# Second mixer of a two-layer decoder trunk: q and k stored in thirds of 32 dimensions, four heads' scores in four quadrants and four PSUM banks, and ScalarE's function tables requested at other places

## The chip, the cores and the metric

The kernel runs on one core of a Trainium2 chip. A core has five engines that run side by side: TensorE (PE: matmuls, and PEld: its weight loads), VectorE (DVE), ScalarE (ACT), GpSimd (POOL) and SyncE (SP), which issues most of the DMAs. Matmuls write to PSUM, which has eight banks of 512 fp32 values for each of 128 partitions. The metric is the device time of one execution in microseconds (us). The kernel before has a median of 994.5 us over 3 runs (994.04 to 995.5).

## The reference, cut to what matters

One sequence of 256 tokens with 1024 features goes through two layers. Each layer is a half-step SwiGLU FFN, a token mixer and another half-step FFN, all with RMSNorm and a shift, scale and gate computed from a condition vector. The first layer's mixer is a block-sparse attention with 16 heads of 64 dimensions and a table of position biases. The second layer's mixer, which the change is about, is a latent attention:

```python
def mla_attention(h, w_dq, q_a_norm_g, w_uq, q_g, w_o, k, v, positions):
    q = (rms_norm(h @ w_dq, q_a_norm_g) @ w_uq).reshape(B, S, MLA_HEADS, MLA_QK)   # 16 heads of 96
    q = rms_norm(q, q_g)
    q = jnp.concatenate([q[..., :MLA_NOPE], rope(q[..., MLA_NOPE:], positions)], axis=-1)   # 64 + 32
    o = causal_block_attention(q, k, v, MLA_QK ** -0.5)
    return o.reshape(B, S, MLA_HEADS * MLA_V) @ w_o
```

The k of a head is built in the same way: 64 dimensions from a latent, 32 position dimensions that all heads share, an RMSNorm over the 96 with gain k_g, and a rotation of the last 32. Scores are q·k over 96 dimensions with a causal mask, softmax runs in fp32, and the output is the weighted sum of v with 64 dimensions a head.

## The kernel before

All activations stay in on-chip memory; only weights are streamed, by SP's queue. Weights and activations are split into a high and a low part in a reduced fp32 format (`fp32r`), and each product is three matmuls: high by high, low by high, high by low (`mm3`, L774 to L776; in most of the FFN L974 and L982). `split` (L644 on ACT, L645 on DVE) makes the two parts of each weight tile. Attention's own matmuls (scores, weighted sum, transposes) are plain fp32, which the chip runs as two instructions for each matmul in the source; transposes are one.

The source text does not give the order of the instructions. Each engine's order comes from a planner in the kernel (`Order`, L250 to L535): it gives every instruction a cost (`duration`, L203), simulates the five engines, and fixes the sequence that each engine then runs strictly in order. So a change of one instruction's cost or buffer can move others.

The second mixer is `mla` (L1408). It works through the 16 heads in four groups of four (`GH` = 4, `NG` = 4), each over the two tiles of 128 query tokens (`t` = 0, 1):

- `proj` makes q for the group (L1483, 128x384), and k and v (L1496, 128x512), into tiles of the ring `mm` (4 banks). `head_rstd` (L1123: ACT L1126, DVE L1129 and L1130, POOL L1131) gives each head's inverse norm; DVE writes the normed heads to `qn` and `kn` (L1486, L1500, L1501), laid out as token x (head, 96), and `rope_apply` rotates the last 32 dimensions.
- `to_T` (L1461) transposes each head on PE (L1466: 128x96 to 96x128, 8 for q and 8 for k in a group) and ACT copies the result with the head gain as a scale for each partition to `qT` and `kT` (L1467).
- `attention` (L1011) is shared by both mixers; `bias is not None` (`halves`) marks the first. `scores` in the second mixer makes three banks of the ring `tr` (3 banks, `at_tile`): one with the four heads' 128x128 scores of tile 0, and two with two heads' 128x256 scores of tile 1. A score is one matmul with 96 rows (L1036); the causal mask is added as a bf16 matmul for each bank (L1037). DVE takes each bank's row maxima (L1050), ACT the exponentials with their sums (L1061), DVE normalises (L1066, L1067).
- `transposes` (L1076) turns the probabilities on PE and ACT copies them (L1078); `av` (L1096) is the weighted sum, two heads side by side in the array's columns, into another bank of `tr`; `split_evac` (L789, L790) writes it out as `oT`.
- `out_proj` (L1107) multiplies `oT` with the output weights.

In the first mixer, scores have 64 rows: the even heads lie on partitions 0 to 63 and the odd ones on 64 to 127, and two heads' matmuls go to different banks (L1041). The ring `ada` (1 bank, `ps_ada`) holds sums for the adaLN gates (L703, L704).

ACT needs a table of functions for Silu and another one for Exp. A load (`ACT_TABLE_LOAD`) stands in the program ahead of the first instruction that needs the other table: Exp's before the first exponential of each mixer (L1061) and Silu's before the first Silu of the FFN after each mixer (L939).

## Time and profile before

The profiled execution took 994.78 us; its span from the first to the last instruction is 993.0 us, and about 1.8 us lie around it.

| Part of the kernel | us from the span's start, about |
|---|---|
| first FFN, with the start and the bias tables | 0 to 213 |
| first mixer | 213 to 328 |
| second FFN | 328 to 514 |
| third FFN (second layer) | 514 to 700 |
| second mixer: latents | 700 to 727 |
| second mixer: four groups of heads | 727 to 790 |
| second mixer: rest of the output projection | 790 to 802 |
| last FFN | 802 to 993 |

The page of a profile lists busy time by engine, the chain of work that ended last (followed backwards from the last instruction), and groups of instructions. A timeline's rows are: start and duration in us, engine, line, operation, output and inputs, how many were merged into the row, and in brackets the idle time before it with what ended it. PE's matmuls overlap in their pipeline, so what one costs is read from start to start and not from its duration.

### The profile page before, as it was taken

What the parts mean: (1) busy time and instruction counts of PE and PEld (TensorE: products, weight loads), DVE (VectorE), ACT (ScalarE), POOL (GpSimd) and SP (SyncE); (2) the same over time, 40 slices, a digit from 0 to 9 for tenths busy, and PEclk for the clock granted to TensorE, in tenths of its full rate; (3) what the DMA queues carried; (4) which work ended last, traced back from release to release, by engine and by line L of the source; (5) the groups of instructions that cost most, each with busy time, mean ns of one, the idle gap of its engine ahead of it and who ended that gap; (6) DMA issues with size and microseconds to landing.
All of it is one profiled execution on the core that took longest, in us unless ns stands there. A gap on an engine that the chain in (4) does not pass through costs nothing.

```text
span 993.0 us, 15266 instructions
## 1 busy us (share of the span) xinstructions
PE 979.3 (99%) x5570; PEld 831.1 (84%) x5573; DVE 842.0 (85%) x1433; ACT 623.1 (63%) x1168; POOL 79.9 (8%) x120
## 2 busy tenths in 40 slices
PE   8999999999999999999999999999999999999998
PEld 7988888878887788888888888888878878888886
DVE  8999999799999999999799999744999789677542
ACT  5698564379665966555367665633879696657421
POOL 1012100012231100000010000000143010000000
PEclk9999999999999999999999999999999999999999
DMA  9978989798887789888989998452343467444630
GB/s 367 408 272 277 363 304 341 288 349 319 297 303 279 250 320 346 321 314 307 366 298 353 351 332 292 171 214 89 106 154 127 171 233 306 181 170 172 230 128 22
DMA packets 53275, 260.55 MB, mean 262 GB/s; under 512 B 6192, under 2 KB 6736, under 8 KB 35024
## 3 DMA queue, kind: packets, MB, share of 16 engines
q1 hardware_dynamic: 51696, 255.93, 70.4%
q0 software_dynamic: 1024, 3.17, 1.0%
q8 instruction: 44, 0.72, 0.3%
q10 hardware_dynamic: 480, 0.47, 0.2%
q14 instruction: 31, 0.25, 0.1%
HBM read 255.36 MB, written 4.19 MB: 261 GB/s over the span
## 4 chain that ended last, share of the span: by engine, by line
PE 84%; DVE 7%; ACT 3%; DMA 3%; issue 1%; POOL 1%; ACTq 0%; SPq 0%; DVEq 0%; POOLq 0%
PE mm L974 23%; PE mm L774 14%; PE mm L775 13%; PE mm L776 13%; PE mm L982 12%; DVE lo L645 3%; DMA raw<-in_first_dram 2%; PE at L1096 1%; PE at L1076 1%; PE at L1036 1%; DMA bias_d<-bt 1%; ACT hi L644 1%; PE at L1041 1%; PE tr L824 1%; PE mm L1623 1%
## 5 line engine op out<-in xcount | busy, mean ns | idle before, releaser
L645 DVE TENSOR_TENSOR lo<-raw,hi 128x1024 fp32r<-128x1024 f32 (+3 forms) x312 | 370.3, 1202 | 79.4 <-ACT hi L644 63.2
L644 ACT ACTIVATE hi<-raw 128x1024 fp32r<-128x1024 f32 (+3 forms) x312 | 318.0, 1038 | 146.9 <-PE mm L776 119.6
L974 PE MATMUL mm<-h,hi 128*128 128x512 f32 x1120 | 288.1, 393 | 0.0
L974 PEld LDWEIGHTS mm<-h,hi 128*128 128x128 f32 x1120 | 199.7, 189 | 34.6
L982 PEld LDWEIGHTS mm<-h,lo 128*128 128x128 f32 x1120 | 155.2, 190 | 12.7 <-DVE lo L645 0.8
L982 PE MATMUL mm<-h,lo 128*128 128x256 f32 x1120 | 162.3, 283 | 0.1
L655 DVE CUSTOM_DVE_ANT_0 adaw<-adaw,c_b,cols 128x1024 f32<-128x1024 f32 x112 | 141.8, 1280 | 3.3 <-DMA adaw<-in_ada_dram 2.3
L774 PE MATMUL mm<-hi,gh 128*128 128x512 f32 x352 | 137.3, 390 | 0.0
L775 PE MATMUL mm<-lo,gh 128*128 128x512 f32 x352 | 137.1, 389 | 0.0
L776 PE MATMUL mm<-hi,gl 128*128 128x512 f32 x352 | 137.1, 389 | 0.0
L774 PE MATMUL mm<-hi,h 128*128 128x512 f32 (+1 forms) x240 | 94.1, 399 | 0.8 <-ACT h L789 0.8
L775 PE MATMUL mm<-lo,h 128*128 128x512 f32 (+1 forms) x240 | 93.2, 393 | 0.0
L776 PE MATMUL mm<-hi,h 128*128 128x512 f32 (+1 forms) x240 | 92.9, 395 | 0.1
L776 PEld LDWEIGHTS mm<-hi,gl 128*128 128x128 f32 x352 | 66.1, 188 | 13.7
L774 PEld LDWEIGHTS mm<-hi,gh 128*128 128x128 f32 x352 | 66.1, 188 | 13.4
L775 PEld LDWEIGHTS mm<-lo,gh 128*128 128x128 f32 x352 | 66.1, 188 | 13.3
L693 DVE SCALAR_TENSOR_TENSOR acc<-adaw,cols,acc 128x1024 f32<-128x1024 f32 x48 | 61.5, 1281 | 0.1
L774 PEld LDWEIGHTS mm<-hi,h 128*128 128x128 f32 x240 | 45.0, 188 | 10.9 <-ACT h L789 1.9
L912 ACT ACTIVATE g<-mm 128x256 f32<-128x256 f32 x70 | 26.4, 377 | 43.7 <-PE mm L982 41.7
L776 PEld LDWEIGHTS mm<-hi,h 128*128 128x128 f32 x240 | 45.0, 188 | 9.5 <-DVE h L790 0.8
L775 PEld LDWEIGHTS mm<-lo,h 128*128 128x128 f32 x240 | 45.1, 188 | 7.7 <-issue 0.2
L912 ACT ACTIVATE u<-mm 128x256 f32<-128x256 f32 x70 | 26.4, 377 | 34.5 <-PE mm L982 34.3
(233 smaller groups left out, 1228.5 us busy)
## 6 DMA issues: line engine op xcount, KB each, us to landing
raw<-in_w_dram SPq DMA_DIRECT2D x142, 1024.0 KB, 5.4
adaw<-in_ada_dram SPq DMA_DIRECT2D x160, 512.0 KB, 5.5
raw<-in_w_dram SPq DMA_DIRECT2D x12, 512.0 KB, 3.6
raw<-in_first_dram SPq DMA_DIRECT2D x7, 512.0 KB, 9.0
raw<-in_w_dram SPq DMA_DIRECT2D x6, 576.0 KB, 3.7
bias_d<-bt SPq DMA_DIRECT2D x12, 256.0 KB, 4.9
bg<-bias_d POOLq DMA_DIRECT2D x4, 768.0 KB, 7.1
raw<-in_first_dram SPq DMA_DIRECT2D x10, 256.0 KB, 9.0
```

What stands on the lines that cost most here:

```text
L644: nc.scalar.activation(hi, src, AF.Copy)
L645: nc.vector.tensor_tensor(lo, src, hi.bitcast(F32), op=ALU.subtract)
L655: nc.vector.tensor_tensor_reduce(wt, wt, c_b, 1.0, cols[:, i, c:c + 1], op0=ALU.mult, op1=ALU.add, accum_out=m_cols[:, i, c:c + 1])
L693: nc.vector.scalar_tensor_tensor(acc, ada_tile(j, k), cact[:, k:k + 1], acc, op0=ALU.mult, op1=ALU.add)
L774: nc.tensor.matmul(ps, lh, rh, start=start, stop=False)
L775: nc.tensor.matmul(ps, lh, rl, start=False, stop=False)
L776: nc.tensor.matmul(ps, ll, rh, start=False, stop=stop)
L824: nc.tensor.transpose(kslice(pt, j), kslice(y, j), ident)
L912: nc.scalar.activation(x, ps[:, S:], AF.Copy)
L974: nc.tensor.matmul(ps[i], w[0], hs[2], start=k == 0, stop=False)
L982: nc.tensor.matmul(ps[i][:, S:], w, hk_, start=False, stop=k == KD - 1)
L1036: nc.tensor.matmul(ps3[:, i, :], qTs(e, t), kTs(e, nk), start=i == 0, stop=False)
```

## The change

- `qn` and `kn` are laid out as token x (third, head, 32) in place of token x (head, 96). A transpose then takes one third of all four heads at once (128x128): head e's 32 dimensions land on partitions 32e to 32e+31, its own quadrant. There are 6 transposes for q and 6 for k in a group, where there were 8 and 8.
- ACT's copies after the transposes: for q three of 128x256 (two with a scale for each partition, one with a constant), for k one of 128x512 and one of 128x256 without a gain. Both gains of the first 64 dimensions are multiplied into q's scale once, ahead of time, in one instruction.
- A score is now three matmuls with 32 rows each, one for each third, summed in PSUM: 24 matmuls in a group in place of 8. The four heads follow each other, each in its own quadrant and its own bank (three of the ring `tr`, the fourth from `mm`), with both query tiles side by side in a head's bank. The mask is added once for each bank, 128x256, four in a group in place of three.
- DVE takes the maxima of a bank by blocks of 128 keys (128x384, four in a group), and two small minima join the two blocks of tile 1 (the values are negated).
- `av` writes to the ring `ada` in place of `tr`, in both mixers.
- A new helper `table` runs one 128x1 activation with scale 0 for its table alone: Exp after the last units of the first FFN of each layer, Silu after the last `av` of each mixer.
- The planner's costs know fp32 matmuls with at most 32 rows (a quarter of the time), and it keeps consecutive ones in their order.

```diff
@@ duration
             c = 2 * max(112.0, cols / 1.2 + 2.5)
-            if DH in (aps[-1].ap[0][1], aps[0].ap[0][1]):
+            rows = aps[0].ap[0][1]
+            if rows <= 32:
+                c /= 4
+            elif DH in (aps[-1].ap[0][1], rows):
                 c /= 2
@@ Order.add
-            half = type(i).__name__ == "InstMatmult" and aps[0].ap[0][1] == DH
+            half = type(i).__name__ == "InstMatmult" and aps[0].ap[0][1] <= DH and i.ins[0].dtype == F32
@@ trunk
+    def table(func, x):
+        nc.scalar.activation(small([P, 1], "none"), x, func, scale=0.0)
@@ ffn
-                    units(f, *ps)
+                    g = units(f, *ps)
+            if idx == 0:
+                table(AF.Exp, g[:, 0:1])
@@ attention, scores
+                ps = [at_tile(), at_tile(), at_tile(), mm_tile()]
+                for e in range(GH):
+                    for t in range(NT):
+                        banks[t, e] = ps[e][:, t * P:(2 * t + 1) * P]
+                for c in range(QK // RO):
+                    for t in range(NT):
+                        for e in range(GH):
+                            nc.tensor.matmul(banks[t, e], qTs(e, t)[c], kTs(e, P * (t + 1))[c],
+                                             start=c == 0 and t == 0, stop=False)
+                for e in range(GH):
+                    ps3 = ps[e][:, :3 * P].rearrange("p (b k) -> p b k", k=P)
+                    nc.tensor.matmul(ps3[:, ::2], ident_b, mask, start=False, stop=True)
+                pe(2.6)
+                mx3, mx = small([P, GH, 3], "mx3"), small([P, GH], "mx")
+                for e in range(GH):
+                    nc.vector.tensor_reduce(mx3[:, e], ps[e][:, :3 * P].rearrange("p (b k) -> p b k", k=P), axis=AX.X,
+                                            op=ALU.max, negate=True)
+                    mxs[0, e], mxs[1, e] = mx3[:, e, 0:1], mx[:, e:e + 1]
+                    if e % 2:
+                        nc.vector.tensor_tensor(mx[:, e - 1:e + 1], mx3[:, e - 1:e + 1, 1], mx3[:, e - 1:e + 1, 2], op=ALU.min)
...
-                for i, e in enumerate(es):
-                    nc.tensor.matmul(ps3[:, i, :], qTs(e, t), kTs(e, nk), start=i == 0, stop=False)
-                nc.tensor.matmul(ps3[:, :, t * P:], ident_b, mask[:, :len(es)], start=False, stop=True)
...
-                    nc.vector.tensor_reduce(mx[:, :len(es)], ps3, axis=AX.X, op=ALU.max, negate=True)
@@ attention, av
-            po = at_tile().rearrange("p (r t q) -> p r t q", r=GH // 2, t=NT)
+            po = (ps_ada.tile([P, 512], F32, tag="ada", name=nm("at"))).rearrange("p (r t q) -> p r t q", r=GH // 2, t=NT)
...
             state["av"] = g + 1
+            if g == NG - 1:
+                table(AF.Silu, oT[0][3][:, kk, 0, 0, 0:1].bitcast(F32))
@@ mla, to_T
-                dst = ap.tile([QK, GH, S], F32, tag=kind + "T", name=nm(kind + "T"))
-                for t in range(NT):
+                dst = ap.tile([P, QK // RO, S], F32, tag=kind + "T", name=nm(kind + "T"))
+                for c0, n in ((0, 2), (2, 1)):
                     pt = tr_tile()
-                    for e in range(GH):
-                        nc.tensor.transpose(pt[:QK, e * P:(e + 1) * P], nat[:, t, e, :], ident)
-                    nc.scalar.activation(dst[:, :, t * P:(t + 1) * P],
-                                         pt[:QK, :].rearrange("p (e q) -> p e q", q=P), AF.Copy, scale=gcol)
+                    for c in range(c0, c0 + n):
+                        for t in range(NT):
+                            nc.tensor.transpose(kslice(pt, 2 * (c - c0) + t), nat[:, t, c].rearrange("p h d -> p (h d)"), ident)
+                    for c in range(c0, c0 + n):
+                        if kind == "q":
+                            nc.scalar.activation(dst[:, c, :], pt[:, (c - c0) * S:(c - c0 + 1) * S], AF.Copy,
+                                                 scale=QK ** -0.5 if c == 2 else places["q"][:, c:c + 1])
+                    if kind == "k":
+                        nc.scalar.activation(dst[:, c0:c0 + n, :], pt[:, :n * S].rearrange("p (c q) -> p c q", q=S), AF.Copy)
@@ mla, groups
-                qn = ap.tile([P, NT, GH, QK], F32, tag="qn", name=nm("qn"), bufs=1)
+                qn = ap.tile([P, NT, QK // RO, GH, RO], F32, tag="qn", name=nm("qn"), bufs=1)
```

More of the change, by code (lines that the diff above doesn't have):

```diff
@@ L1025, in scores @@
             for t, es in UNITS:
                 nk = P * (t + 1)
-                ps = at_tile()
-                ps3 = ps.rearrange("p (e k) -> p e k", k=nk)
+                s3 = ap.tile([P, 512], F32, tag="w", name=nm("s"), bufs=5).rearrange("p (e k) -> p e k", k=nk)
+                ss.append(s3)
                 if halves:
-                    odd = mm_tile()[:, :2 * P].rearrange("p (e k) -> p e k", k=P) if t == 0 else None
-                    banks.append([(odd if odd is not None and e % 2 else ps3)[:, e // 2, :] for e in es])
-                    continue
@@ L1033, in scores @@
-                banks.append(ps3)
-                for i, e in enumerate(es):
-                    nc.tensor.matmul(ps3[:, i, :], qTs(e, t), kTs(e, nk), start=i == 0, stop=False)
-                nc.tensor.matmul(ps3[:, :, t * P:], ident_b, mask[:, :len(es)], start=False, stop=True)
-            for t in range(NT if halves else 0):
-                for e in range(GH):
-                    u = 1 + e % 2 if t else 0
-                    nc.tensor.matmul(banks[u][UNITS[u][1].index(e)], qTs(e, t), kTs(e, P * (t + 1)),
-                                     start=True, stop=True)
@@ L1350, in rope_tables @@
             cossin[nme] = w_
-    gcols, tabs = [], []
-    mask = cp.tile([P, GH, P], BF16, name="mask")
+    tabs = []
+    mask = cp.tile([P, NT, P], BF16, name="mask")
     def mla_consts():
@@ L1473, in to_T @@
                     qT, kT = then["q"], then["k"]
-                    attention(ap, g, lambda e, t: qT[:, e, t * P:(t + 1) * P], lambda e, n: kT[:, e, :n],
+                    attention(ap, g, lambda e, t: [qT[e * RO:(e + 1) * RO, c, t * P:(t + 1) * P] for c in range(QK // RO)],
+                              lambda e, n: [kT[e * RO:(e + 1) * RO, c, :n] for c in range(QK // RO)],
                               lambda e, kb: vs[g][:, kb, e * DH:(e + 1) * DH], None, oT, state)
@@ L1504, in mla @@
                 state["v"] = g + 1
-                later(TK_WAIT, lambda g=g, kn=kn, then=then: to_T(g, "k", kn, gcols[1], then))
+                later(TK_WAIT, lambda g=g, kn=kn, then=then: to_T(g, "k", kn, then))
             out_proj(oT, (1, 1), after)
```

78 lines of the change are left out of this document (41 added, 37 removed).

## Prediction, written before the changed kernel ran

> **What bounds the kernel now.** I read the page first, then the busy time by stretches of the second mixer, then PE's timeline there.
>
> ```profile
> PE 979.3 (99%) x5570; PEld 831.1 (84%) x5573; DVE 842.0 (85%) x1433; ACT 623.1 (63%) x1168; POOL 79.9 (8%) x120
> PE 84%; DVE 7%; ACT 3%; DMA 3%; issue 1%; POOL 1%; ACTq 0%; SPq 0%; DVEq 0%; POOLq 0%
> ```
>
> PE is busy for 99% of the span and carries 84% of the chain of waits. So an instruction taken from PE is time gained, unless another engine takes PE's place in that stretch. In 735 to 780 us, where three of the four head groups have their scores, the sum of three stretches and the stretch behind them are:
>
> ```profile
> sum 45.00, PE 44.15 PEld 37.59 DVE 42.10 ACT 40.28 POOL 14.79; mean PE 14.72 PEld 12.53 DVE 14.03 ACT 13.43 POOL 4.93
> ...
> 780.00:795.00 15.00, 15.00 (x92) 12.31 (x91) 8.54 (x15) 8.32 (x25) 0.00 (x0) 1.00 0.39 147
> ```
>
> PE leads with 44.15 of 45 us, but DVE has only 2.9 us free here; behind 780 us it has 6.5 us of 15 free. PE's own timeline of the first group's softmax and the second group's scores:
>
> ```profile
> 742.74 1.08 PE L1466 MATMUL tr<-ident,qn 128*96 128x128 f32 x8 [0.50 <-ACT s L1061]
> 744.00 1.19 PE L1466 MATMUL tr<-ident,kn 128*96 128x128 f32 x8 [0.18 <-ACT s L1061]
> 745.12 1.80 PE L1076 MATMUL at<-ident,s 128*128 128x128 f32 x12
> 746.85 1.75 PE L1096 MATMUL at<-pT,v 128*64 128x128 f32 x24
> 748.53 2.24 PE L1036 MATMUL at<-kT,qT 96*128 96x128 f32 x12
> 750.61 0.27 PE L1037 MATMUL at<-mask,ident_b 128*128 128x256 bf16 x1
> 750.72 1.03 PE L1036 MATMUL at<-kT,qT 96*128 96x256 f32 x4
> 751.58 0.27 PE L1037 MATMUL at<-mask,ident_b 128*128 128x256 bf16 x1
> 751.61 0.48 PE L774 MATMUL mm<-hi,ckT 128*128 128x512 f32 x1
> ...
> 757.43 1.47 PE L1076 MATMUL at<-ident,s 128*128 128x128 f32 x12
> 758.65 0.42 PE L774 MATMUL mm<-hi,qlT 128*128 128x384 f32 x1
> ...
> 761.69 1.58 PE L1096 MATMUL at<-pT,v 128*64 128x128 f32 x24
> 763.20 2.24 PE L1036 MATMUL at<-kT,qT 96*128 96x128 f32 x12
> ```
>
> Three things are to be seen. Scores and masks of a group hold PE from 748.53 to 751.61, 3.08 us. Transposes follow each other at 1.22 / 12 = 0.10 us where nothing delays them (757.43 to 758.65). And the first group loses time: 0.50 and 0.18 us of idle time, 1.73 us for twelve transposes (745.12 to 746.85) where the next group takes 1.22, and 1.68 us for the weighted sum where the next group takes 1.51. That is 0.50 + 0.18 + 0.51 + 0.17 = 1.36 us.
>
> **The change part by part.** *Scores.* Four instructions with 256 columns take 0.86 us (750.72 to 751.58), 0.215 each. A 256-column mask takes 0.11 (750.61 to 750.72); the masks stream 1024 columns a group before and after, 0.44 us, and cancel. So the 16 score instructions (8 matmuls, two instructions each) cost 3.08 - 0.44 = 2.64 us a group. The change makes them 48, with 32 rows each. What four in separate quadrants cost, this trace does not show; the nearest rows are the first mixer's scores, where two heads lie in separate halves:
>
> ```profile
> 241.01 0.39 PE L776 MATMUL mm<-hi,h 128*128 128x512 f32 x1
> 241.33 0.37 PE L1041 MATMUL at<-kT,qT 64*128 64x128 f32 x1
> 241.34 0.37 PE L1041 MATMUL mm<-kT,qT 64*128 64x128 f32 x1
> ...
> 241.66 0.27 PE L1041 MATMUL at<-kT,qT 64*128 64x128 f32 x1
> 241.66 0.27 PE L1041 MATMUL mm<-kT,qT 64*128 64x128 f32 x1
> 241.77 0.27 PE L1041 MATMUL at<-kT,qT 64*128 64x128 f32 x1
> ...
> 241.88 1.03 PE L1041 MATMUL at<-kT,qT 64*128 64x256 f32 x8
> 242.84 0.50 PE L774 MATMUL mm<-hi,h 128*128 128x512 f32 x1
> 243.18 0.40 PE L775 MATMUL mm<-lo,h 128*128 128x512 f32 x1
> 243.41 0.39 PE L776 MATMUL mm<-hi,h 128*128 128x512 f32 x1
> ```
>
> Two heads' instructions start within 0.01 us of each other, and the next pair 0.11 us later: the pair costs what one costs. Eight of 256 columns are through in 0.96 us, four times 0.215 and a changeover of 0.10. So halves run side by side in full. Without any overlap, a third of the dimensions costs 4 heads x 2 instructions x (0.11 + 0.215) = 2.6 us, a group 7.8 us. Overlapped twofold that is 3.9, fourfold 1.95. These are the bounds; I take 1.95, because the rows show no loss at all in going from one to two. Gain: 4 x (2.64 - 1.95) = 2.76 us. The changed kernel's order takes some back: in the first group three heads' first scores stand apart, with ten fp32r matmuls before the fourth head's, and in the last group one head's stands apart. Each costs another pass of 2 x 0.11 us. Net gain 2.3 us (bounds: 2.76, and a loss of 5.5 at twofold).
>
> *Transposes.* 12 a group in place of 16: 16 x 0.10 = 1.6 us gained. Twelve is what a full 128x128 form takes at 0.10 in the row above, so this has no open bound. ACT's copies read 1536 columns a group in 5 instructions in place of 2048 in 4, which is no more work than before.
>
> *Changeovers.* From fp32r to scores PE's step is 0.32 us (241.01 to 241.33), and behind them 0.34 (242.84 to 243.18), where the plain step is 0.23 (243.18 to 243.41): an excursion costs 0.2 us. By the two orders, PE leaves the fp32r stream 105 times before and 111 times after. I count 6 x 0.2 = 1.2 us lost (bounds: 0, if they are short runs of transposes whose entry is free, and 2).
>
> The Trainium skill (TensorEngine Tiling (Array Packing), Tiling Modes, Key Properties) says that changing the tiling mode drains the engine, which speaks against small tiles with full-height masks behind them. The trace agrees in kind, with the 0.10 us just shown; before, scores of 96 rows and masks share a mode. By that rule the four groups' masks cost 4 x 0.1 us more, an estimate, and the sum below would be 0.4 us smaller.
>
> *The tables.* ACT in the first group, and DVE's rows that price the maxima:
>
> ```profile
> 738.82 0.49 ACT L1126 ACTIVATE sq<-mm 128x384 f32<-128x384 f32 x1 [0.99 <-DVE hv L1129]
> 739.32 1.28 ACT L1061 ACT_TABLE_LOAD   x1
> 740.61 0.37 ACT L1061 ACTIVATE s<-at,mx 128x128 f32<-128x128 f32 x1
> ...
> 794.13 0.63 ACT L803 ACTIVATE ry<-x 128x512 f32<-128x512 f32 x1 [4.07 <-DVE x L884]
> ```
>
> ```profile
> 726.39 0.15 DVE L1441 TENSOR_SCALAR spe<-spe 128x1 f32<-128x1 f32 x1
> ...
> 738.73 0.69 DVE L1050 TENSOR_REDUCE mx<-at 128x4 f32<-128x512 f32 x1
> ...
> 758.50 0.55 DVE L1129 TENSOR_REDUCE hv<-sq 128x4 f32<-128x384 f32 x1
> ...
> 773.79 4.75 DVE L645 TENSOR_TENSOR lo<-raw,hi 128x1024 fp32r<-128x1024 f32 x4
> ```
>
> The first maxima are there at 739.42, the first exponential starts at 740.61: the load costs 1.19 us on the way to PE, which waits for banks that the exponentials free. Early, it stands in an FFN. Of the 1.36 us lost in this group I take 1.0 back (bounds 0 and 1.36): the exponentials now begin only when all 24 score matmuls of the group are done, where the first bank used to be ready after a third, and that keeps a part. The Silu load moves to the idle time of 4.07 us on ACT ahead of 794.13 and stands ahead of no waiting work there; Silu's old place cost PE no wait worth counting. If that cover were gone, ACT's queue would shift by 1.28 us.
>
> *Maxima.* 16 of 0.55 in place of 12 of 0.69, and 8 small minima at some 0.15: +0.5 + 1.2 = 1.7 us on DVE over four groups, beside PE's work as long as DVE has its free 2.9 us.
>
> *Banks.* The weighted sum leaves the ring `tr`, and the fourth head's scores enter the ring `mm`: projections queue behind that bank until its exponentials end. The planner has put other matmuls there, and I count nothing; its price is among the rivals.
>
> Sum: -2.3 - 1.6 + 1.2 - 1.0 = -3.7 us. The profiled execution took 994.78, so 991.1; the median of the runs is 994.5, 0.3 lower, so **990.8 us**.
>
> **The rivals.**
>
> *Threefold overlap.* Four quadrants may share something that two halves do not need. At threefold a group takes 7.8 / 3 = 2.6 us in place of 1.95: 2.6 us lost on four groups, sum -1.1, 993.4 us. For it: no row shows four; against it: the two halves lose nothing. The Trainium skill (TensorE: Matmul & The Clock Gate, Measured speedup vs the span model) gives 3.07 for four row tiles of 32; by it the group takes 2.54 us, an estimate, and the sum is -1.3.
>
> *Twofold overlap, the other side.* If only two quadrants run at a time, the group takes 3.9 us, more than the 2.64 now: 7.8 us worse than my forecast, sum +4.1, 998.6 us, slower. It decides from where a group passes 1.95 + 3.7 / 4 = 2.9 us, an overlap of 2.7. For it: 48 weight loads in place of 16, with 32 rows each; against it: the pair's loads cost no step of their own above. With no overlap at all it would be 1014.
>
> *Gain lost to waits.* DVE has 42.1 us of work in 45 and gets 1.3 more for three groups: the stretch can shrink by 1.6 us and no more, unless the four splits at 773.79 (4.75 us, for weights of later matmuls) slip behind 780, where there is room. The fourth head's bank in `mm` works the same way. Then about 992.9. For it: 94% busy; against it: the splits can move.
>
> *Better than forecast.* Changeovers cost nothing and all of 1.36 comes back: -5.3, and with fewer waits in the latents some 988.5.
>
> **How the numbers follow.** Forecast 0.55 (its own range 989 to 992.4), threefold 0.13, waits 0.15, twofold or worse 0.10, better 0.07. Within 0.2%, 992.5 to 996.5, is what a measurement of this kernel cannot tell from no change. Faster: 0.53 of the forecast, 0.07, and 0.08 of threefold and waits, 0.68. Same: the rest of these and a little of the twofold, with an overlap just under three, 0.21. Slower: 0.11. The range leaves out the twofold case above and the best below: 988.3 to 995.5.
>
> **What would show it.** Right: a group's score run of 48 instructions, masks and all, in 2.4 to 2.6 us, four starts within some 0.03 us of each other at steps of 0.11 and 0.215; no table load between the first maxima and the first exponential, and the 0.50 us of idle time on PE ahead of the q transposes gone; twelve transposes of q and k a group at 0.10. Wrong: quadrants at steps of 0.2 us or more; PE idle in the groups above 1 us, released by DVE's maxima or by a bank of `mm`; DVE at 15 of 15 us in the stretches.

## The result, and the profile after

The changed kernel takes 999.69 us (median of 4 runs, 999.29 to 1000.32); the kernel before, in runs beside it, 994.71 us (994.04 to 995.5). The ratio is 1.0051, with a 95% interval of 1.0039 to 1.0063: 5.0 us slower where 3.7 us faster was forecast, and outside the range of 988.3 to 995.5. The profiled execution of the changed kernel took 1000.02 us, with a span of 998.3.

The page of the changed kernel, its busy times and its chain:

```profile
PE 982.2 (98%) x5689; PEld 829.7 (83%) x5689; DVE 843.8 (85%) x1445; ACT 623.6 (62%) x1176; POOL 80.0 (8%) x120
...
PE 82%; issue 9%; DVE 5%; ACT 2%; POOL 1%; DMA 1%; SPq 0%; POOLq 0%; ACTq 0%
```

PE still carries the chain, but "issue" has gone from 1% to 9% of it: time in which an engine waited for nothing that the chain could name. The busy time by stretches says where. First the sum of 735 to 780 us and the stretch behind it, as shown of before, and then the sum over all four stretches (735 to 795 us) after, and under it that of before:

```profile
sum 45.00, PE 42.48 PEld 32.42 DVE 39.73 ACT 37.63 POOL 13.30; mean PE 14.16 PEld 10.81 DVE 13.24 ACT 12.54 POOL 4.43
...
780.00:795.00 15.00, 15.00 (x136) 11.92 (x134) 12.24 (x19) 8.46 (x23) 0.00 (x0) 1.00 0.58 211
...
sum 60.00, PE 57.48 PEld 44.34 DVE 51.97 ACT 46.09 POOL 13.30; mean PE 14.37 PEld 11.09 DVE 12.99 ACT 11.52 POOL 3.33
```
```profile
sum 60.00, PE 59.15 PEld 49.90 DVE 50.64 ACT 48.60 POOL 14.79; mean PE 14.79 PEld 12.48 DVE 12.66 ACT 12.15 POOL 3.70
```

No other engine is busy throughout: DVE and ACT are less busy in 735 to 780 us than before (DVE 39.73 where it had 42.10, ACT 37.63 where it had 40.28), and over all four stretches DVE has 51.97 where it had 50.64. PE itself now stands idle for 2.5 of 60 us, where it stood for 0.85.

The scores do what was forecast. PE's timeline of the second group, from the first score to the last mask:

```profile
751.60 0.39 PE L1054 MATMUL at<-kT,qT 32*128 32x128 f32 x3
751.62 0.37 PE L1054 MATMUL mm<-kT,qT 32*128 32x128 f32 x1
751.81 0.28 PE L1054 MATMUL at<-kT,qT 32*128 32x128 f32 x3
...
751.92 0.39 PE L1054 MATMUL at<-kT,qT 32*128 32x256 f32 x3
...
752.14 0.39 PE L1054 MATMUL at<-kT,qT 32*128 32x256 f32 x3
...
753.47 0.37 PE L1054 MATMUL mm<-kT,qT 32*128 32x256 f32 x1
753.78 0.50 PE L777 MATMUL mm<-hi,ckT 128*128 128x512 f32 x1
754.12 0.50 PE L1058 MATMUL at<-mask,ident_b 128*128 128x256 bf16 x3
754.46 0.27 PE L1058 MATMUL mm<-mask,ident_b 128*128 128x256 bf16 x1
754.49 0.48 PE L778 MATMUL mm<-lo,ckT 128*128 128x512 f32 x1
```

Four heads start within 0.02 us of each other, and later ones follow after 0.11 us (128 columns, 751.81 to 751.92) and after 0.22 us (256, 751.92 to 752.14): fourfold overlap. The 48 score instructions take 2.18 us (751.60 to 753.78) and the masks 0.37 (754.12 to 754.49), 2.55 us where the group took 3.08. But look at what follows: the softmax starts only with the masks, its first maximum at 754.44. These are the maxima and the first and the last exponential of that group:

```profile
754.44 1.49 DVE L1062 TENSOR_REDUCE mx<-at 128x3 f32<-128x384 f32 x3 [0.41 <-PE at L1058]
755.84 0.55 DVE L1062 TENSOR_REDUCE mx<-mm 128x3 f32<-128x384 f32 x1
```
```profile
755.03 0.37 ACT L1081 ACTIVATE s<-at,mx 128x128 f32<-128x128 f32 x1 [0.49 <-DVE mx L1062]
...
758.92 0.52 ACT L1081 ACTIVATE s<-mm,mx 128x256 f32<-128x256 f32 x1
```

DVE waits for the mask, ACT for DVE. The first exponential starts 0.57 us behind the start of the last mask and the last one ends at 759.44, so the group's banks are held from 751.60 to 759.44, 7.84 us. The kernel before, in its third group, the first and the last exponential:

```profile
765.34 0.37 ACT L1061 ACTIVATE s<-at,mx 128x128 f32<-128x128 f32 x1
...
768.86 0.47 ACT L1061 ACTIVATE s<-at,mx 128x256 f32<-128x256 f32 x1
```
```profile
765.28 0.27 PE L1037 MATMUL at<-mask,ident_b 128*128 128x256 bf16 x1
...
766.99 0.28 PE L1037 MATMUL at<-mask,ident_b 128*128 128x256 bf16 x1
```

There the first bank's maxima and exponentials ran beside the scores of the other two banks: the first exponential started 1.65 us ahead of the last mask. The scores began at 763.20 (a row of the prediction), so from the first score to the last exponential it is 6.13 us, with three banks, of which the first is given back after its four exponentials. So the banks are four now in place of three, and held longer.

Where this becomes idle time on PE is seen first in the first group of the changed kernel:

```profile
734.85 0.76 PE L1054 MATMUL at<-kT,qT 32*128 32x128 f32 x6
...
738.61 0.37 PE L1054 MATMUL mm<-kT,qT 32*128 32x128 f32 x1
...
741.70 0.39 PE L1054 MATMUL at<-kT,qT 32*128 32x128 f32 x3
...
742.91 0.27 PE L1058 MATMUL mm<-mask,ident_b 128*128 128x256 bf16 x1
...
744.44 0.34 PE L779 MATMUL mm<-hi,qlT 128*128 128x384 f32 x1
745.10 1.24 PE L1495 MATMUL tr<-ident,qn 128*128 128x128 f32 x6 [0.32 <-ACT s L1081]
...
747.44 0.44 PE L1495 MATMUL tr<-ident,kn 128*128 128x128 f32 x2 [0.42 <-ACT qT L1498]
748.17 1.19 PE L1096 MATMUL at<-ident,s 128*128 128x128 f32 x8 [0.29 <-ACT qT L1498]
749.53 0.63 PE L1096 MATMUL at<-ident,s 128*128 128x128 f32 x4 [0.17 <-ACT pT L1098]
```
```profile
743.48 0.37 ACT L1081 ACTIVATE s<-at,mx 128x128 f32<-128x128 f32 x1 [0.71 <-DVE mx L1062]
...
747.24 0.51 ACT L1081 ACTIVATE s<-mm,mx 128x256 f32<-128x256 f32 x1
```

Three heads' first scores open the three banks of `tr` at 734.85; the fourth head follows at 738.61, the last third at 741.70. The exponentials run from 743.48 to 747.75. The next group's q transposes need a bank of `tr`: they wait until an exponential has freed one (the bracket at 745.10), and what stands behind them on PE waits for ACT's copies of those same few banks (747.44, 748.17, 749.53). There is no table load in between any more, and the first exponential is still 2.87 us later than before (740.61).

To see how much each step gave, I went through all starts of PE from the first matmul of the K/V latents to the first of the last FFN. Each step from start to start is split into the plain step of its kind and what is over it; more than 0.25 us over is called a stall:

| us | before | after | difference |
|---|---|---|---|
| scores and masks | 12.46 | 11.16 | -1.30 |
| transposes | 16.86 | 15.32 | -1.54 |
| fp32r matmuls and weighted sums (a few records are missing before) | 89.70 | 90.57 | +0.87 |
| changeovers from and to fp32r (74 and 92), and between other kinds | -0.43 | 2.18 | +2.61 |
| stalls (7 and 17) | 4.03 | 8.99 | +4.96 |
| all | 122.61 | 128.21 | +5.60 |

(Of the changeovers' difference 2.0 us are at the fp32r stream. They sum to less than nothing before because a transpose's last plain step falls into the fp32r matmul behind it; only the difference means something.) The loss is in the stalls, and half as much again in the changeovers.

Not all of the stalls are at the banks. Of the 8.99 us, 3.63 lie in the latents, ahead of the first score (2.38 before), and 0.63 behind the groups (0.63 before). In the groups there are 4.73, where the kernel before has 1.01. Of these, 2.2 us lie between 744.44 and 749.53, in the rows just shown, nearly all behind an exponential or one of ACT's copies, and 1.1 have no named wait (ahead of 734.85, 736.11 and 775.38). The last 1.5 (ahead of 759.67, 774.45 and 776.38) are waits for DVE, for heads' norms and for normalised probabilities. Two of them:

```profile
759.67 0.41 PE L1495 MATMUL tr<-ident,qn 128*128 128x128 f32 x2 [0.34 <-DVE hv L1152]
...
776.38 0.63 PE L1096 MATMUL at<-ident,s 128*128 128x128 f32 x4 [0.36 <-DVE s L1087]
```

### The profile page after: what moved, and what is told of

Its sections match the earlier page's. It is cut to its first block, busy times and chain, and to the rows that moved or that the text cites. A ratio compares the mean times of both kernels' runs of the same rounds, so it can differ in the third digit from the quotient of the medians.

```text
span 998.3 us, 15527 instructions
## 1 busy us (share of the span) xinstructions
PE 982.2 (98%) x5689; PEld 829.7 (83%) x5689; DVE 843.8 (85%) x1445; ACT 623.6 (62%) x1176; POOL 80.0 (8%) x120
## 4 chain that ended last, share of the span: by engine, by line
PE 82%; issue 9%; DVE 5%; ACT 2%; POOL 1%; DMA 1%; SPq 0%; POOLq 0%; ACTq 0%
PE mm L982 23%; PE mm L990 12%; PE mm L777 12%; PE mm L778 12%; PE mm L779 12%; PE at L1116 1%; PE at L1096 1%; PE mm L1657 1%; PE tr L1217 1%; DVE lo L648 1%; PE mm L1659 1%; PE mm L1658 1%; PE at L1054 1%; PE tr L827 1%; DMA raw<-in_first_dram 1%
## 5 line engine op out<-in xcount | busy, mean ns | idle before, releaser
L777 PEld LDWEIGHTS mm<-hi,h 128*128 128x128 f32 x240 | 45.1, 188 | 10.8 <-ACT h L792 1.8
L814 POOL TENSOR_TENSOR rstd<-ssq,mhalf 128x1 f32<-128x1 f32 x12 | 13.5, 1124 | 413.6 <-DVE ssq L809 347.6
```

Source lines behind the costliest of these rows:

```text
L777: nc.tensor.matmul(ps, lh, rh, start=start, stop=False)
L814: nc.gpsimd.tensor_tensor(r, stats[t], mhalf[:, 0:1], op=ALU.pow)
```

## The experiments

Six theories were made after the result, some of them on the way. A: projections queue behind the fourth head's bank in `mm`. B: the banks of the scores, opened together and freed late, are what PE's queue waits for. C: the thirds themselves cost (copies, strided multiplications, 32-row loads). D: the order before is a lucky draw of the planner, which any edit loses. M: the chain from scores by maxima to exponentials, which no longer runs beside the scores. L: a reordering by the planner in the latents. Times are medians; the kernel before, run beside each of them, had 994.7 to 995.1 us.

### The parts of the change

*Tables alone*, and *all but the tables*:

```diff
 kernel before
+            if idx == 0:
+                table(AF.Exp, g[:, 0:1])
...
+            if g == NG - 1:
+                table(AF.Silu, oT[0][3][:, kk, 0, 0, 0:1].bitcast(F32))
```

> The kernel before with the early table requests alone. My prediction's term: 0 to 1.36 us faster than before, about 993.7. Rival (the planner's fixed order shifts with any edit, and that is what costs): some other difference, up to 1.5 us slower, with no table load on the path.

> The changed kernel without the early table requests (loads at their old places). If the requests are worth the 1 us that I gave them: 1000.7. If the changed kernel's first group waits for its fourth bank and not for the table, the load is hidden anyway or hurts in full: 999.7 to 1001. If the early requests are what spoils the order: 998 or less.

Tables alone: 996.05 us (ratio 1.0015, 1.0005 to 1.0024). All but the tables: 999.85 us (1.0051, 1.0036 to 1.0066), the same as with them. In the changed kernel the loads are indeed early; ACT's group of them:

```profile
L898 ACT ACT_TABLE_LOAD x4 | 5.1, 1283 | 0.1
```

Four loads of 1.28 us each, with 0.1 us of idle time before them in all, at the places where the change put them. In time they gave nothing. The trace of the tables alone shows that the term did what was forecast where it was forecast: PE is busy for 60.00 of the 60 us of the four stretches, and the first group's 1.0 us of stalls is gone. But the stalls in the latents are 4.2 us there in place of 2.4. Why the tables alone cost 1.2 us isn't settled: the profiled execution is the shortest of the ten (995.07), and its last matmul is only 0.15 us later than before.

*The banks.* The fourth head in `ada` with the weighted sum back in `tr`, and the weighted sum alone back in `tr`:

```diff
 changed kernel
-                ps = [at_tile(), at_tile(), at_tile(), mm_tile()]
+                ps = [at_tile(), at_tile(), at_tile(), ps_ada.tile([P, 512], F32, tag="ada", name=nm("at"))]
...
-            po = (ps_ada.tile([P, 512], F32, tag="ada", name=nm("at"))).rearrange("p (r t q) -> p r t q", r=GH // 2, t=NT)
+            po = at_tile().rearrange("p (r t q) -> p r t q", r=GH // 2, t=NT)
```

> The changed kernel with the fourth head's scores in the ring ada and the weighted sum in tr, as before. Theory A (the fourth head's bank in the ring mm makes the first group's scores wait, 3.8 us between the third and the fourth head's first scores): 3 to 4 us faster than the changed kernel, 996. Theory B (all four banks are freed late by the exponentials, whatever ring they are in): 999 to 1000.

> The changed kernel with the weighted sum back in the ring tr, the fourth head's scores still in mm. Theory A: as the changed kernel, 999 to 1001. Theory B (the ring tr is what is short): 1 to 2 us slower, above 1001, since tr then has to hold one more tile.

The first gave 1006.29 us, the second (the last two lines alone) 1003.37 us. The first has both edits, so it is to be compared with the second: with the weighted sum in `tr` in both, taking the fourth head out of `mm` costs 2.9 us more, where theory A expects a gain. That speaks against A but does not settle it, since the one bank of `ada` brought a wait of its own: from the third group's first score to the fourth group's last exponential 24 us go by there (771.96 to 795.93). A fourth user of `tr` in each group costs 3.7 us, more than the 1 to 2 us that B expects, and in its direction.

*The bank of the weighted sum alone, on the kernel before*, and *the whole bank layout alone*:

```diff
 kernel before
-            po = at_tile().rearrange("p (r t q) -> p r t q", r=GH // 2, t=NT)
+            po = (ps_ada.tile([P, 512], F32, tag="ada", name=nm("at"))).rearrange("p (r t q) -> p r t q", r=GH // 2, t=NT)
```

> The kernel before with one line of the change: the weighted sum takes its bank from the ring `ada` in place of `tr`. Theory B (ring `tr` with its three banks is what the second mixer waits for): putting it back cost the changed kernel 3.7 us, so here a bank more for every group is worth something, 991 to 994.5 us, and nothing gets slower. Theory D (the order by which the planner fills PE changes with every edit, and its luck is worth some us): any time from 991 to 999, with no wait on a `tr` bank to explain it.

```diff
 the same, and
+                ps = [at_tile(), at_tile(), at_tile(), mm_tile()]
...
+                for t in range(NT):
+                    for e in range(GH):
+                        nc.tensor.matmul(banks[t, e], qTs(e, t), kTs(e, P * (t + 1)), start=t == 0, stop=False)
+                for e in range(GH):
+                    ps3 = ps[e][:, :3 * P].rearrange("p (b k) -> p b k", k=P)
+                    nc.tensor.matmul(ps3[:, ::2], ident_b, mask[:, :NT], start=False, stop=True)
```

> The kernel before with the changed kernel's banks, and nothing else of it: a head's two tiles of scores in one bank, three banks of `tr` and one of `mm`, all 8 matmuls and 4 masks before the first maximum, maxima by head with the minima, the weighted sum in `ada`. Heads keep 96 rows: no quadrants, no thirds, 16 transposes. Theory B (the loss comes from banks that all come free late): slower than before, 998 to 1004 us; at its fullest it is the changed kernel's 999.7 and the 3.9 us that packing and transposes then gave. Theory C (the loss comes from the thirds: copies, strided multiplications and 32-row loads): within 0.2% of before, 993 to 996.5 us.

The weighted sum in `ada` alone: 997.33 us (1.0025, 1.0016 to 1.0034). B's expectation is missed, for B had nothing slower; D allows for it, without a reason. PE's timeline of its third group shows one; under it the weighted sum of the kernel before:

```profile
775.74 0.43 PE L1096 MATMUL at<-pT,v 128*64 128x128 f32 x2
776.10 0.50 PE L775 MATMUL mm<-lo,h 128*128 128x512 f32 x1
...
776.76 0.43 PE L1096 MATMUL at<-pT,v 128*64 128x128 f32 x2
...
779.39 1.36 PE L1096 MATMUL at<-pT,v 128*64 128x128 f32 x20
```
```profile
776.26 1.58 PE L1096 MATMUL at<-pT,v 128*64 128x128 f32 x24
```

With a bank of its own the weighted sum begins early and in pieces (2, 2 and 20 instructions, 775.74 to 780.7) between fp32r matmuls, and each piece pays for its changeovers; before, it went through in one run of 1.5 us. That this is all of the 2.4 us was not tried.

The whole layout with 96-row scores, so without quadrants, thirds and tables: 998.13 us (1.0031, 1.0020 to 1.0041), 3.3 us slower than before. This is at the low end of what theory B expects, and C isn't needed for it: the loss is there without any thirds. But it isn't in stalls: by the account above they are 4.0 us, as before, while the changeovers take some 2 us more (84 from and to fp32r, where before had 74). There the layout costs by breaking PE's order into shorter pieces. Of the 3.3 us the weighted sum's bank alone had 2.4; but put back, it cost the changed kernel 3.7, so the parts don't add up singly.

### Releasing the banks earlier

*Exponentials by head*, then also the probabilities' transposes in that order:

```diff
 changed kernel
-            for u, (t, es) in enumerate(UNITS):
...
+                for u, i in ((0, 0), (1, 0), (0, 1), (1, 1), (0, 2), (2, 0), (0, 3), (2, 1)):
+                    ex(u, i)
+                    if (u, i) in ((1, 1), (0, 3), (2, 1)):
+                        norm(u)
```

> The changed kernel with the eight exponentials of a group in the order of heads (tile 0 and tile 1 of head 0, then of head 1, and so on), so that the banks come free after 2, 4, 6 and 8 exponentials in place of 5, 6, 7 and 8. The work is the same. Theory B: the first bank comes free three exponentials, some 1.1 us, earlier in each of four groups, 996 to 998.5 us. If the time that matters is that of the first normalized probabilities and not of the banks, they are ready later and it is 999.5 to 1002.

> As the run with exponentials by head, and the probabilities' transposes take the units in the order in which they are normalized (heads 0 and 1 of tile 1, then tile 0, then heads 2 and 3 of tile 1). Theory B: 995.5 to 998.5 us, at least as fast as exponentials by head alone. If the banks are not what is waited for: 999 to 1001.

By head: 998.24 us, 1.45 us faster than the changed kernel with the same work, a time that B expects. Its trace does not show B's way to it, though. From the first score to the last exponential the first and the third group take as long as without it (12.9 and 7.7 us), the second longer (9.5 in place of 7.8) and only the fourth less (7.1 in place of 10.8), because the planner no longer splits that group's scores. The stalls in the second and the third group fell from 1.8 to 0.4 us. With the transposes in that order too: 1000.15 us, B's expectation missed. In that run the planner has split the scores of the fourth group again (12.0 us from first score to last exponential, where by head alone had 7.1).

### Is it only the order?

Every step of a group is put into the program some us of PE work behind the one before it, by constants (S for scores, PT for the probabilities' transposes, AV for the weighted sum, TQ and TK for the transposes of q and k); they had been set for the kernel before. Two kernels with other waits before, and two after:

```diff
 second mixer alone
-        later(S_WAIT, scores)
+        later(S_WAIT if halves else 1.4, scores)
...
-            later(PT_WAIT, transposes)
+            later(PT_WAIT if halves else 7.3, transposes)
```

> The kernel before with other waits in the second mixer alone (S 1.4, PT 7.3, AV 3.7, TQ 4.1, TK 5.0 us in place of 2.4, 5.0, 2.6, 5.4, 4.6): the same instructions and banks in another order on PE. Theory D (the order before is a lucky draw: the two one-step edits so far, tables and the bank of the weighted sum, both made it slower without a mechanism of their own): 996 to 999 us, though the planner's own end is earlier than that of before. Theory B (banks that come free late): no banks are changed, 993 to 996 us.

> As the run before it, with S 1.7, PT 4.5, AV 1.7, TQ 3.9, TK 5.5 us. Theory D: 996 to 999 us. Theory B: 993 to 996 us.

> The changed kernel with other waits in the second mixer alone (S 1.9, PT 4.1, AV 2.8, TQ 4.1, TK 3.4 us), the best of some 45 orders by the planner's own costs, 2.4 us ahead of the changed kernel there. Theory D: the change was measured with waits that were set for the other kernel, and with its own it gains; 994 to 997.5 us. Theory B: banks are held as long in any order; 998.5 to 1001 us.

> The changed kernel with exponentials by head (998.24 us with the old waits) and other waits in the second mixer alone (S 2.5, PT 5.9, AV 2.3, TQ 4.5, TK 3.2 us). Theories B and D together: banks come free earlier and the order is its own, 993.5 to 996.5 us. Theory B alone: as with the old waits, 997.5 to 999 us.

Before with other waits: 993.80 us (0.9989, 0.9979 to 0.9998) and 994.43 us (0.9997, 0.9988 to 1.0006). Two other orders do as well or better, so the kernel before is not the one lucky draw that theory D takes it for. An order can still be worth some us: the tables alone and the weighted sum's bank alone lost 1.2 and 2.4. After with other waits: 998.32 us; by head and other waits: 996.93 us (1.0022, 1.0012 to 1.0031). Both lie between the range expected with D and the one by B alone. Its own waits give the changed kernel 1.3 to 1.4 us, and the rest of its loss stays. The first of these runs is the fastest kernel of the study; its four stretches have no idle time on PE:

```profile
sum 60.00, PE 60.00 PEld 51.23 DVE 50.70 ACT 49.46 POOL 13.64; mean PE 15.00 PEld 12.81 DVE 12.67 ACT 12.37 POOL 3.41
```

### The chain to the exponentials

*No maxima*, after and before. These two leave out the row maxima that keep the softmax in range, so they compute another function and serve the timing alone:

```diff
 changed kernel; the kernel before accordingly
-                    nc.vector.tensor_reduce(mx3[:, e], ps[e][:, :3 * P].rearrange("p (b k) -> p b k", k=P), axis=AX.X,
-                                            op=ALU.max, negate=True)
...
-                                         bias=mxs[t, e], scale=-1.0 if halves else 1.0,
+                                         bias=mxs[t, e] if halves else 0.0, scale=-1.0 if halves else 1.0 / 64,
```

> The changed kernel without the second mixer's maxima and minima; its exponentials take scores / 64 and no bias. It leaves the stabilization of the softmax out and computes another function; exponentials, banks, transposes and matmuls are as many and as large. Theory M (the loss is the softmax chain: all four heads' scores end together, so that maxima and exponentials no longer run beside the scores but behind the last mask, 0.57 us behind it where they began 1.65 and 2.07 us ahead of it before): 994.5 to 997 us. Theory B alone (banks held, whatever the maxima): 998.5 to 999.7 us.

> The kernel before without the second mixer's maxima, exponentials of scores / 64 without a bias: the same is left out. Its maxima already run beside its scores, so Theory M gives little: 993.5 to 995 us, and the changed kernel is then within 2 us of it where it is 4.9 us slower with maxima. Theory B: both gain the same, and the distance stays 4 to 5 us.

After: 995.24 us (1.0003, 0.9993 to 1.0012); before: 995.43 us (1.0005, 0.9996 to 1.0014). Without maxima the changed kernel gains 4.45 us and the kernel before nothing, and the two are level. The second group of the changed kernel without maxima, first score, exponentials, and the four stretches:

```profile
751.12 0.39 PE L1054 MATMUL at<-kT,qT 32*128 32x128 f32 x3
...
753.98 0.27 PE L1058 MATMUL mm<-mask,ident_b 128*128 128x256 bf16 x1
```
```profile
753.96 0.28 ACT L1074 ACTIVATE s<-at 128x128 f32<-128x128 f32 x1 [0.43 <-PE at L1058]
...
756.80 0.41 ACT L1074 ACTIVATE s<-mm 128x256 f32<-128x256 f32 x1
```
```profile
sum 60.00, PE 59.35 PEld 47.92 DVE 46.71 ACT 45.61 POOL 14.03; mean PE 14.84 PEld 11.98 DVE 11.68 ACT 11.40 POOL 3.51
```

ACT starts as soon as the masks are there and is through at 757.21, so the banks are held for 6.09 us in place of 7.84, and PE's idle time in the four stretches falls from 2.5 to 0.65 us. The stalls in the groups fall from 4.7 to 1.5 us; those for DVE are gone, and those in the latents are as before (3.6). After, this is theory M's expectation; before, 995.43 is 0.4 us above its range, but the distance between the two kernels closes as M has it, where B alone keeps it. It does not part DVE's time from ACT's: without a bias the exponentials are shorter too (0.28 us in place of 0.37 for 128 columns), in both kernels.

*Masks first*, to shorten the chain without taking work from DVE or ACT; and with by-head order and waits of its own:

```diff
 changed kernel
+                for e in range(GH):
+                    ps3 = ps[e][:, :3 * P].rearrange("p (b k) -> p b k", k=P)
+                    nc.tensor.matmul(ps3, ident_b, mask, start=True, stop=False)
...
-                                             start=c == 0 and t == 0, stop=False)
-                for e in range(GH):
-                    ps3 = ps[e][:, :3 * P].rearrange("p (b k) -> p b k", k=P)
-                    nc.tensor.matmul(ps3[:, ::2], ident_b, mask, start=False, stop=True)
+                                             start=False, stop=c == 2 and t == NT - 1)
...
```

> The changed kernel with the four masks ahead of a group's scores in place of behind them (each mask now covers all 384 columns of its bank and opens it, the scores are added to it). The last score is then all that the maxima wait for: in the changed kernel the last mask starts 0.99 us behind the last score (753.47 to 754.46), so maxima begin some 0.9 us earlier in each group, for 128 columns more of mask a head on TensorE. Theory M (the chain from scores by maxima to exponentials is what the group waits for): 996 to 998.5 us. If the chain is not what is waited for: 999.5 to 1000.5 us.

> Masks first, exponentials by head, and the second mixer's own waits (S 0.8, PT 5.7, AV 2.6, TQ 4.4, TK 3.6 us), the best of some 100 orders by the planner's costs. Theory M and the waits together: 992.5 to 995.5 us, no slower than the kernel before. If a shorter chain adds nothing to by-head and waits: 996.5 to 997.5 us.

Masks first: 1001.14 us, 1.45 slower than the changed kernel. All together: 997.18 us (1.0021, 1.0012 to 1.0030), no better than by head and waits alone. Both expectations of M are missed. The second group of masks first, on PE and ACT:

```profile
750.05 0.33 PE L1053 MATMUL mm<-mask,ident_b 128*128 128x384 bf16 x1
...
753.60 0.34 PE L1053 MATMUL at<-mask,ident_b 128*128 128x384 bf16 x1
...
755.74 0.37 PE L1057 MATMUL mm<-kT,qT 32*128 32x256 f32 x1
```
```profile
756.52 0.37 ACT L1081 ACTIVATE s<-at,mx 128x128 f32<-128x128 f32 x1 [0.87 <-DVE mx L1062]
...
760.37 0.49 ACT L1081 ACTIVATE s<-mm,mx 128x256 f32<-128x256 f32 x1
```

The chain did become shorter: from the start of the last score to the first exponential 0.78 us (755.74 to 756.52) where the changed kernel has 1.56 (753.47 to 755.03). But the masks need nothing, so the planner issued them as soon as a bank was free, one at a time from 750.05 to 753.60, and each opened its bank. From the first mask to the last exponential it is now 10.81 us. By the account of starts the shorter chain did take waiting away: the stalls are 6.9 us, 2.1 fewer than in the changed kernel. What made it slower is work on PE. Scores and masks take 1.8 us more (a mask covers 384 columns in place of 256, and the scores stand in more pieces), and the changeovers 1.8 more. So this run does not show that the chain is without weight, nor that the longer hold alone costs the time.

### An exchange in the latents

In the changed kernel PE waits longer in the latents, which the change does not touch:

```profile
703.34 0.32 PE L777 MATMUL mm<-hi,hkv 128*128 128x288 f32 x1
704.62 0.44 PE L779 MATMUL mm<-hi,h 128*128 128x384 f32 x1 [0.97 <-DVE h L793]
```

```diff
 after the planner, on DVE's order
+        x = next(j for j, s in enumerate(name) if s.startswith("hkv_"))
+        y = next(j for j in range(x, len(d)) if name[j].startswith("h_"))
+        d[x], d[y] = d[y], d[x]
```

> The changed kernel with one pair of VectorE instructions in the latents exchanged, back to the order that the kernel before has there: a quarter of the FFN's next input (h) ahead of the K/V latents' input (hkv). TensorE waits 1.16 us for that h at 703.34 in the changed kernel and 0.30 there before. Theory L (part of the loss is this reordering by the planner, in work that the change does not touch): 998.3 to 999 us. Rival (the wait is made up later, in waits that come anyway): 999.4 to 1000 us.

> The changed kernel with exponentials by head and its own waits (996.93 us) and the pair of VectorE instructions in the latents exchanged. Theory L: 995.5 to 996.3 us. Rival (the wait is made up later): 996.7 to 997.2 us.

1000.05 and 997.22 us, the same as without the exchange (999.69 and 996.93). The wait at 703.34 went, but another of 0.97 us came at 704.43, for a later part of the same input. So theory L isn't borne out, though a kernel without that wait was not tried.

### All of them by the time that banks are held

For each kernel, the time from the first score or mask of a group to the end of its last exponential, summed over the four groups, read as in the rows above. These are the kernels in which a group holds four banks, three of `tr` and one of `mm`, with the weighted sum in `ada`:

| kernel | held, us | time, us |
|---|---|---|
| after, no maxima | 29.9 | 995.24 |
| by head, other waits | 32.7 | 996.93 |
| by head, other waits, exchange in the latents | 32.8 | 997.22 |
| before with the bank layout alone | 36.2 | 998.13 |
| after, other waits | 37.0 | 998.32 |
| by head | 37.2 | 998.24 |
| after | 39.3 | 999.69 |
| after, exchange in the latents | 39.3 | 1000.05 |
| after, no tables | 39.6 | 999.85 |
| masks first, by head, other waits | 41.0 | 997.18 |
| exponentials and transposes by head | 42.3 | 1000.15 |
| masks first | 45.7 | 1001.14 |

The hold is that of the profiled execution, the time a median. The time rises with the hold, about 0.37 us for each us from the first row to the last (5.9 over 15.8), but loosely: the row of 41.0 lies 2 us below that line. There a single mask opens the bank of `mm` 5.1 us ahead of the second group's others (746.14 and 751.28). The table alone also doesn't say which is the cause: whatever holds PE up inside a group lengthens the hold too, and these kernels differ in PE's work and in their changeovers besides. With three banks there is no such line: before holds them for 26.4 us at 994.9, with other waits 28.0 at 993.80 and 25.2 at 994.43, with the tables alone 23.7 at 996.05, with the weighted sum in `ada` 25.5 at 997.33, without maxima 19.9 at 995.43. The weighted sum back in `tr` (37.4 us, 1003.37) lies off the line, as another user of the short ring, and so does the fourth head in `ada`, whose scores wait open.

Open stays why the changed kernel without maxima ends level with the one before and not 4 us ahead. In the account by starts it still has 5.1 us of stalls, where the kernel before without maxima has 1.8. Of these 3.3 us more, 1.8 lie in the latents, ahead of any score, and 1.5 in the groups. So the waits in the latents, which theory L was about, are a part of the difference that no run here explains.

## Why the prediction was wrong

**The step that failed is the banks**: "projections queue behind that bank until its exponentials end. The planner has put other matmuls there, and I count nothing." I looked at the one bank in `mm` and at who queues behind it there, and beside it I took the maxima for hidden. The price was on the other three banks: all of `tr` is opened by one group at once and given back only behind the maxima, and the softmax of a group no longer runs beside its scores. Two runs show that this costs what the prediction put at nothing. The layout alone, without any of the gains, lost 3.3 us; and the maxima taken out gave the changed kernel 4.45 us back, and the kernel before nothing.

How it reaches PE is shown only in part. Stalls rose by 4.96 us, 3.7 of them in the groups, which alone takes up the whole forecast of 3.7. About 1.2 of these 3.7 are at `tr` and its copies (2.2 us, where before had 1.0), 1.5 are waits for DVE and 1.1 have no named wait. Another 1.25 us are in the latents, and their cause stays open. And the layout alone lost its 3.3 us without more stalls, mostly in changeovers. That the hold of the banks is the one thing behind all of this is argued, not shown.

- *Scores, -2.3.* The mechanism was right in each sign: fourfold overlap, starts within 0.02 us, 2.55 us for a group with masks (2.4 to 2.6 forecast). The sum was mis-sized: scores and masks gave 1.30 us, since the runs of the first and the fourth group come in pieces, each with its own entry. The Trainium skill (TensorE: Matmul & The Clock Gate, Measured speedup vs the span model) gives 3.07 for four row tiles of 32, with 512 columns. The second group here, with 128 and 256 columns, has 7.8 us of instructions (the prediction's sum without overlap) in 2.09 (751.60 to 753.47 and the last 0.22). That is 3.7, so this trace does not agree with it, and the measurement decides.
- *Transposes, -1.6.* Right: -1.54.
- *Changeovers, +1.2.* Nine more excursions (74 to 92 crossings) in place of six. Those at the fp32r stream cost 2.0 us more, the upper bound, and those between other kinds 0.6. The weighted sum in pieces, which a free bank allows, was not in the count.
- *Tables, -1.0.* Wrong for this kernel. Alone, the early load did take the first group's 1.0 us of waits away. In the changed kernel the load left its place, but the first exponential moved from 740.61 to 743.48, because it waits for a third of q and k that the planner placed last (741.70). Two runs put the tables' worth in time at nothing, or at a loss. The sentence that "the exponentials now begin only when all 24 score matmuls of the group are done" named the cause, and priced it as a part of 1.36 us in one group, where it stretched the hold in all four.
- *Maxima, +1.7, hidden.* Counted as DVE's throughput, and over the four stretches DVE does have 8 us free. Their cost is latency: they stand in one lump behind the masks (754.44 to 756.39), where the exponentials wait for them, the banks with these, and DVE's next norms behind them. In the kernel before the same work is free (without it, 995.43).
- *The rivals.* Threefold, twofold and worse were excluded by the rows. "Gain lost to waits" had the direction, but capped the loss at the gain. A wait that a new layout adds has no such cap.

## What to carry to other kernels

Before work is packed so that several results end together, see which results used to end first, and what ran behind them in the meantime: a consumer that overlapped with its producer is lost as cover, and what it had given back early is held until the end. Ask of a buffer ring how long its banks are held, from the first write to the last read, and what else has to pass through it; the time of the instructions does not tell. Before a table of runs is read as a cause, split one of its rows by where the engine waits and where it works: here a kernel that was slower had less waiting. A constant retuned on the old kernel is a cheap control: it showed here that the loss was not only the planner's luck, and gave the only version that was faster, by 1 us.

## What was not expected of the hardware

An exponential without a bias operand takes 0.28 us for 128x128 from PSUM where one with a bias for each partition takes 0.37 (753.96 without maxima, 755.03 with them), and 0.41 where it takes 0.52 for the last 128x256 of the group (756.80 and 758.92). So dropping the maxima also made ACT some 0.1 us faster for each of 32 exponentials. The Trainium skill (ScalarE: Activation LUTs, What ACT_TABLE_LOAD costs) gives about 93 ns for such an operand, and this trace agrees.
